# A two-layer decoder trunk on one core: one convolution put off less, another not at all, and one pair of sevens less in two down panels

## The chip, the cores and the metric

The kernel runs on one NeuronCore of a Trainium2 chip. Its engines work side by side, each through its own list of instructions: TensorE (PE in the profile; PEld is its weight load) multiplies matrices, VectorE (DVE) and ScalarE (ACT) do elementwise work, GpSimd (POOL) and SyncE (SP) issue transfers. The metric is the device time of one execution in microseconds (us), as the median of several.

## The reference

What is computed is a trunk of two layers over 256 tokens of width 2048, in float32. The first layer mixes the tokens with gated linear attention, the second with forgetting attention, and both attend to 256 memory tokens. After the mixer, each layer runs the same feed-forward block, and the change lies in that block alone:

```python
def causal_dwconv(u, w, b):
    s_ = u.shape[1]
    up = jnp.pad(u, ((0, 0), (CONV_WIDTH - 1, 0), (0, 0)))
    return w[0] * up[:, 0:s_] + w[1] * up[:, 1:s_ + 1] + w[2] * up[:, 2:s_ + 2] + b

def conv_ffn(h, w_up, conv_w, conv_b, w_down):
    u = causal_dwconv(h @ w_up, conv_w, conv_b)
    a, val = split_cols(u, [FFN_HIDDEN, FFN_HIDDEN])
    return (jax.nn.silu(a) * val) @ w_down
```

The hidden width is 5632, which is 44 chunks of 128. `w_up` is 2048 x 11264 and `w_down` 5632 x 2048, for each of the two layers.

## The kernel before

**Numbers in two parts.** Each float32 operand is split into a high part that the matmul takes as it is, and a low part, the rest. A product is three matmuls (high with high, low with high, high with low). Inputs are kept split. Weights are split as they come in: SP loads a unit of 128 x 1024 into a slot `raw`, ScalarE copies it to a slot `whi` (line 256), VectorE subtracts to get `wlo` (line 257). The slots form rings, in the feed-forward block eight for `raw` and six each for `whi` and `wlo`, so a split of a later unit has to wait until TensorE has used up an older one. Some slots are lent and carry other names (`moremk`, `moremv`, `more`).

**Panels and steps.** An "up" panel j makes four chunks of the hidden width (j to j+3) for both halves: 16 units, one for each chunk of the input. A "down" panel takes the finished chunks of one part and adds to two of the four 512-wide quarters of the output. The parts are chunks 0 to 15, 16 to 27 and 28 to 43 (`PARTS`, line 33), so down panels have 16, 12 and 16 units. The order in each layer is: up 0, 4, 8, 12 and, one panel ahead, up 16; two down panels of the first part; up 20, 24 and, ahead, up 28; two down panels of the second part; up 32, 36, 40; then the last part's down panels. The two down panels of a part are the wide ones: f = 0 for the first half of the output, f = 2 for the second. A step is one unit, and an ordinary one is 12 matmuls of 128 x 512.

**Pairs of sevens.** `pair_steps` (line 408) can take two neighbouring units together with seven block products instead of eight, in the manner of Strassen and Winograd: 21 matmuls in place of 24. For that it needs sums of the two input chunks (`usum` and `dsum`, made once) and of the weights. The weights of a pair are four splits, one of 512 and three of 1024 columns (`split_more`, lines 404 and 405), and four differences on VectorE (lines 461 to 464); two of the four splits wait for them. The seven products are collected in other banks than the ordinary ones, and after the last pair of a panel they are added to the result (`early`; for a down panel three additions and five that go to x, lines 1372 to 1382). Each up panel has a pair at chunk 6 and those of `MORE_IN` another. In down panels the chunks 4, 10, 20 and 34 begin a pair (`SEVEN_DOWN`, line 36). `ONCE` (line 43) picks which pair the first wide panel of a part takes: chunk 10 in the first part, chunk 20 in the second. The second wide panel takes all pairs of its part: 4 and 10 in the first part, 20 in the second.

**The convolution.** It runs along the tokens, while the up panel leaves the tokens in the partitions. So each half panel (`turn`, line 1481) is transposed in blocks on VectorE, sent to DRAM and fetched back on POOL's queue (lines 674 and 679), and only then convolved: 12 taps on ScalarE (line 1442), two additions (line 1449), the gate (line 1455), the product (line 1462) and the split into the chunk's two parts (lines 552 and 553), which writes the ring `m` of 16 chunks. These are listed as small steps with a cost each, 10.2 for a half panel and 20.4 for a panel. `tick` (line 1504) is called after each unit: it adds a share to a credit (1.45, in up panels with two pairs 1.7; a step of a pair counts as a tick but adds nothing) and issues steps in order while the credit lasts. A half panel's steps come due a number of ticks after its up panel: 8, or 7 for the first half where the next up panel has two pairs. `PUT_OFF` (line 42) replaces that number for panels 16 and 28, with 30 and 22. For panel 16 some delay is needed: its chunks go into the places of chunks 0 to 3 in the ring, which the first part's down panels still read, as their first four units. Panel 28's chunks go into places that the second part does not read.

**Order.** The program's order is rearranged by a planner that simulates the engines; the splits of weights have 300 instructions of priority (`AHEAD`, line 50), so they are issued well before the matmuls that need them, and a tap is kept behind the last of these splits. Each engine then runs its list in order.

Of the kernel before, what the change touches and what calls it, by code (L numbers as in the profile page):

```python
# [38 lines left out]
SCRATCH = 2048  # L39
SLOTS = 5  # L40
RAW_GUESTS = 3
PUT_OFF = {16: 30, 28: 22}
ONCE = {0: 10, 1: 20}


LEVELS = (64, 16, 4)
# [105 lines left out]
def _trunk(ctx: ExitStack, tc: tile.TileContext, xt, xtok, memt, wp, wgu, gns, gfin, cnv, par, msk, out):  # L152
# [367 lines left out]
    def add_to(f):  # L520

        return lambda b, a: V.tensor_tensor(x[f][:, b, :], x[f][:, b, :], a, ALU.add)
# [847 lines left out]
    def down_pair(l, p, f, src, sums, flip, pool, temps, then=None):  # L1370

        def early(bank):
            t0, t1 = temps()
            S.activation(t0, bank["p1"], AF.Copy)
            add_to(f)(0, t0)
            V.tensor_tensor(t0, bank["p6"], t0, ALU.add)
            V.tensor_tensor(t1, bank["p7"], t0, ALU.add)
            add_to(f)(1, t1)
            add_to(f + 1)(1, t1)
            add_to(f + 1)(1, bank["p5"])  # L1380
            V.tensor_tensor(t0, bank["p5"], t0, ALU.add)
            add_to(f + 1)(0, t0)

        def late(b, h, a):
            held_back = then is not None and h and not b and then.rooms is not None
            with tc.issue_after(then.turned[-1].ins) if held_back else nullcontext():
                add_to(f + h)(b, a)
            if then is not None:
                then(f + h, b)

        return pair_steps(where["down", l, p, f], src, sums, flip, pool, early, late)
# [26 lines left out]
    def ffn(l, nx, h, m, more, ys, zs, landing, then, pool, temps, last=None, spare=None):  # L1418
        with tc.tile_pool(name=f"ffn{l}", bufs=1) as fp:
# [14 lines left out]
            count = [0, 0, 0]  # L1434
            sums = {}
# [45 lines left out]
            def turn(j, wait):  # L1481

                count[0] += 1
                slot = count[0] % 2
                y, z = ys[slot], zs[slot]

                def evac(b, a):
                    with tc.high_priority(offset=AHEAD):
                        turned_last[0] = V.transpose(y[:, :, :, b, :], a.rearrange("p (k c i) -> p c k i", c=4, i=32))
                    if b:  # L1490
                        away = far_away(dram, flat(y), T, nc.gpsimd)
                        back = lambda: away(flat(z))
                        steps = [(0.5, lambda s=s, c=c, i=i: tap_of(j, s, c, i, slot)) for n in ((1, 2), (0,))
                                 for s in range(2) for c in range(2) for i in n]
                        steps += [(1.0, lambda: add_tap(1)), (1.0, lambda: add_tap(2)), (0.5, silu),
                                  (1.0, lambda: gated(j, 0)), (0.7, lambda: gated(j, 1))]
                        returns.append((clock[0] + 3, slot, back, [(clock[0] + wait, *step) for step in steps]))

                return evac
# [4 lines left out]
            def tick(share):  # L1504

                clock[0] += 1
                credit[0] = min(credit[0], 0.0) + share
                while returns and returns[0][0] <= clock[0] and not unread[returns[0][1]]:
                    _, slot, back, steps = returns.pop(0)
                    back()  # L1510
                    unread[slot] = 12
                    waiting.extend(steps)
                while waiting and waiting[0][0] <= clock[0] and credit[0] > 0:
                    _, cost, step = waiting.pop(0)
                    credit[0] -= cost
                    step()

            def up_pair(j):

                count[2] += 1  # L1520
                second = j // 4 in MORE_IN
                turns = [turn(j + 2 * h_, PUT_OFF.get(j) or (7 if not h_ and j // 4 + 1 in MORE_IN else 8)) for h_ in range(2)]
                u = {}
# [27 lines left out]
            def drive(steps, share=1.45):  # L1551
                for k in steps:
                    tick(share if k >= 0 else 0.0)

            def drive_up(j):
                drive(up_pair(j), 1.7 if j // 4 in MORE_IN else 1.45)
# [6 lines left out]
            for p, (lo, hi) in enumerate(PARTS[:-1]):  # L1563
                while done < hi + 4:
                    drive_up(done)
                    done += 4
                src = [m[c % RING] for c in range(lo, hi)]
                for f in (0, 2):
                    count[2] += 1
                    drive(down_pair(l, p, f, src, {c - lo: t for c, t in sums.items() if f or c == ONCE[p]}, count[2] % 2, pool,  # L1570
                                    lambda: (temps(0), temps(1))))
                sums.clear()
            lo, hi = PARTS[-1]
# [3 lines left out]
            p = len(PARTS) - 1  # L1577
            src = [m[c % RING] for c in range(lo, hi)]
# [86 lines left out]
    with tc.tile_pool(name="stash", bufs=1) as st:  # L1665
        vt = st.tile([P, 2, FOX_H * HD], F32, name="fvt")
        turned3 = vt.rearrange("p b t -> p (b t)").rearrange("p (f q k b j) -> p f q k b j", f=3, q=4, k=4, b=2)
        turned3 = [turned3[:, f] for f in range(3)]

        with tc.tile_pool(name="turn1", bufs=1) as tp:  # L1670
            n2, then = preparing("kv", bufB, tp, dram, turned3, "raw2", nc.gpsimd)
            ys = [const.tile([P, 4, 4, 2, 32], F32, name="yu", tag=tag) for tag in ("mk0", "mv0")]
            fixed = [vt.rearrange("p b t -> p (b t)")[:, 2048 + 512 * i : 2560 + 512 * i] for i in range(2)]

            def temps(i):
                return fixed[i] if i < 2 else tp.tile([P, 512], F32, name="temp", tag=f"temp{i}")

            more = []
            for t, tag in ((mk, "mk1"), (mv, "mv1")):
                parked.append(dram.tile([P, 4 * T], F32, name="park" + tag, tag="park" + tag, bufs=1))  # L1680
                nc.gpsimd.dma_start(parked[-1], t[1].rearrange("p a b -> p (a b)"))
                more.append(const.tile([P, NUNIT], F32R, name="more" + tag, tag=tag))
            ffn(0, n, bufB, bufA, more, ys, turned3, ys, then, tp, temps)
        fox(n2, vt, turned3)
# [9 lines left out]
    with tc.tile_pool(name="store", bufs=1) as op:  # L1694
# [16 lines left out]
        def then(f, b):  # L1711
            fin.add(f, b)
            if f == 0 and b == 0:
                S.activation(junk, fin.sums[:, 0, 0:1], AF.Sqrt)
            V.tensor_tensor(x[f][:, b, :], x[f][:, b, :], gf[f], ALU.mult)
# [37 lines left out]
        then.begin, then.rooms = begin, None  # L1753
        more = [op.tile([P, NUNIT], F32R, name=f"more{i}") for i in range(2)]
        ffn(1, n, bufA, bufB, more, ys, zs, zs, then, op, temps, last, spare)


# [68 lines left out]
```

## Time and profile before

| | |
|---|---|
| median of 3 runs | 2220.16 us (2220.07 to 2223.7) |
| the profiled execution's own time | 2225.07 us |
| its span, first to last instruction | 2223.3 us |
| busy: TensorE, VectorE, ScalarE, GpSimd | 99%, 83%, 65%, 6% |
| first feed-forward block, up to the last wide panel | from 456.6 to 1083.1 us of the span |
| second feed-forward block, the same | from 1502.2 to 2126.0 us |

The profile is that of one execution, so its stretches add up to its span, and not to the median. TensorE's busy share is counted from modelled ends of overlapping matmuls; whether it stood still is better seen in the time from one matmul's start to the next. In the rows of the profile, "out<-in" names what an instruction writes and reads, a number after x is a count, and square brackets give the idle time of the engine before the instruction with what ended it.

### The profile page before, as it was taken

Reading aid. Unit: us, or ns where it says so; the run is one execution under the profiler, and the core shown is the slowest. Engines: PE = TensorE matmul, PEld = TensorE weight load, DVE = VectorE, ACT = ScalarE, POOL = GpSimd, SP = SyncE. Lnnn points to the kernel's source line nnn. Section 1 sums busy time; section 2 is a strip of 40 time slices with the busy share of each in tenths; the row PEclk is TensorE's granted clock in tenths of the full one; section 3 lists DMA queues with packets and bytes.
Section 4 is the critical chain, followed back from the end, with each engine's and each line's share of the span. In section 5 each row is a group of like instructions: output and inputs, shape, how many; then the busy total and the mean of one; then the engine's idle time right before and its main releaser. Section 6 shows DMA issues by size and latency. Waiting matters only on the chain.

```text
span 2223.3 us, 30061 instructions
## 1 busy us (share of the span) xinstructions
PE 2198.0 (99%) x10273; PEld 1840.9 (83%) x10273; DVE 1853.4 (83%) x2771; ACT 1440.0 (65%) x2292; POOL 136.7 (6%) x257
## 2 busy tenths in 40 slices
PE   9999999999999999999999999999999999999998
PEld 7888888888888878887788998888888887888786
DVE  7768976689998889899887669668999888989896
ACT  6655655557784667656865555455887466766784
POOL 0000000001100000001110000000101000100100
PEclk9999999999999999999999999999999999999999
DMA  9766667777776567656777767776787657675682
GB/s 366 252 224 214 201 208 232 249 236 248 256 261 218 184 213 269 220 196 232 259 230 245 226 201 244 226 243 230 257 272 235 221 166 256 225 243 200 237 285 93
DMA packets 166289, 515.40 MB, mean 232 GB/s; under 512 B 20780, under 2 KB 42552, under 8 KB 166136
## 3 DMA queue, kind: packets, MB, share of 16 engines
q1 hardware_dynamic: 149064, 460.99, 61.9%
q0 software_dynamic: 16496, 51.71, 7.3%
q8 instruction: 80, 1.31, 0.2%
q10 hardware_dynamic: 576, 0.79, 0.1%
q14 instruction: 73, 0.60, 0.1%
HBM read 469.62 MB, written 43.79 MB: 231 GB/s over the span
## 4 chain that ended last, share of the span: by engine, by line
PE 92%; DVE 3%; ACT 2%; DMA 2%; issue 1%; POOL 0%; DVEq 0%; ACTq 0%; POOLq 0%
PE acc L361 26%; PE acc L434 26%; PE ps_s L434 14%; PE ps_o L434 7%; PE ps_t L434 6%; PE acc L332 3%; PE acc L287 3%; PE ps_s L361 2%; PE acc L391 2%; PE acc L285 1%; DMA raw<-wp 1%; ACT whi L256 1%; DVE wlo L257 1%; DVE wlo L405 1%; ACT tap L1442 1%
## 5 line engine op out<-in xcount | busy, mean ns | idle before, releaser
L257 DVE TENSOR_TENSOR wlo<-raw,whi 128x1024 fp32r<-128x1024 f32 (+2 forms) x610 | 725.6, 1198 | 198.3 <-ACT whi L256 181.0
L256 ACT ACTIVATE whi<-raw 128x1024 fp32r<-128x1024 f32 (+2 forms) x610 | 629.6, 1043 | 402.9 <-PE acc L361 141.6
L361 PE MATMUL acc<-whi,B 128*128 128x512 f32 (+3 forms) x1248 | 290.8, 369 | 0.0
L361 PEld LDWEIGHTS acc<-whi,B 128*128 128x128 f32 x1248 | 226.8, 188 | 28.1
L405 DVE TENSOR_TENSOR wlo<-raw,whi 128x1024 fp32r<-128x1024 f32 (+1 forms) x164 | 176.5, 1084 | 35.9 <-ACT whi L404 22.9
L404 ACT ACTIVATE whi<-raw 128x1024 fp32r<-128x1024 f32 (+1 forms) x164 | 154.6, 949 | 75.8 <-PE acc L434 20.4
L434 PE MATMUL acc<-whi,B 128*128 128x512 f32 x654 | 175.2, 390 | 1.4 <-ACT whi L256 1.4
L434 PE MATMUL acc<-whi,mix 128*128 128x512 f32 x620 | 163.9, 390 | 0.3 <-ACT whi L256 0.3
L361 PE MATMUL acc<-wlo,B 128*128 128x512 f32 (+3 forms) x624 | 159.0, 369 | 0.0
L434 PEld LDWEIGHTS acc<-whi,B 128*128 128x128 f32 x654 | 122.4, 188 | 28.4 <-ACT whi L256 2.9
L434 PEld LDWEIGHTS acc<-whi,mix 128*128 128x128 f32 x620 | 116.0, 188 | 26.0 <-ACT whi L256 2.0
L1442 ACT ACTIVATE tap<-fvt,cw 128x256 f32<-128x256 f32 x264 | 122.5, 530 | 17.7 <-DMA fvt<-far 10.8
L1442 ACT ACTIVATE tap<-yzu,cw 128x256 f32<-128x256 f32 x264 | 122.5, 529 | 16.8 <-DMA yzu<-far 10.0
L361 PEld LDWEIGHTS acc<-wlo,B 128*128 128x128 f32 x624 | 114.2, 188 | 14.7
L1449 DVE TENSOR_TENSOR tap<-tap,tap 128x1024 f32<-128x1024 f32 x88 | 106.8, 1214 | 0.0
L434 PE MATMUL ps_s<-whi,mix 128*128 128x512 f32 x360 | 103.9, 389 | 0.0
L434 PE MATMUL acc<-wlo,B 128*128 128x512 f32 x327 | 99.9, 390 | 0.8 <-DVE wlo L257 0.8
L434 PE MATMUL acc<-wlo,mix 128*128 128x512 f32 x310 | 92.8, 390 | 1.5 <-DVE wlo L257 1.5
L434 PE MATMUL ps_s<-whi,B 128*128 128x512 f32 x278 | 80.6, 389 | 0.0
L434 PEld LDWEIGHTS ps_s<-whi,mix 128*128 128x128 f32 x360 | 67.6, 188 | 14.0
L434 PEld LDWEIGHTS acc<-wlo,B 128*128 128x128 f32 x327 | 61.2, 188 | 14.2 <-DVE wlo L257 1.6
L361 PE MATMUL acc<-whi,mix 128*128 128x512 f32 x280 | 70.2, 390 | 0.0
(557 smaller groups left out, 4317.9 us busy)
## 6 DMA issues: line engine op xcount, KB each, us to landing
raw<-wp SPq DMA_DIRECT2D x741, 512.0 KB, 4.5
fvt<-far POOLq DMA_DIRECT2D x100, 128.0 KB, 4.9
raw<-wp SPq DMA_DIRECT2D x32, 384.0 KB, 3.6
far<-yu POOLq DMA_DIRECT2D x22, 512.0 KB, 3.6
far<-yzu POOLq DMA_DIRECT2D x22, 512.0 KB, 3.4
yzu<-far POOLq DMA_DIRECT2D x88, 128.0 KB, 4.4
raw<-wp SPq DMA_DIRECT2D x24, 388.0 KB, 3.6
x<-xtok SPq DMA_DIRECT2D x8, 512.0 KB, 7.1
```

The costliest lines, as they stand in the source:

```text
L256: casts.append(S.activation(hi[:, s], raw[:, s], AF.Copy))
L257: lows.append(V.tensor_tensor(lo[:, s], raw[:, s], hi[:, s].bitcast(F32), ALU.subtract))
L285: mm = TE.matmul(acc[p][c][:, :T], w[:, s], both[:, 0, :], start=False, stop=end and j == 3)
L287: mm = TE.matmul(acc[p][c], w[:, s], both, start=u == j == 0, stop=end and j == 3)
L332: mm = TE.matmul(acc[b][:, :n], src[kcs[j] - base][:, part, b * P : (b + 1) * P], w, start=u == 0 and low == part == j == 0, stop=u == end ...
L361: mm = TE.matmul(acc[b][:, :n], src[kc - base][:, part, b * P : (b + 1) * P], ready[low][:, j * room : j * room + n], start=i == low == pa ...
L391: mm = TE.matmul(acc[b][:, :n], src[kc - base][:, part, b * P : (b + 1) * P], w, start=i == low == part == j == 0, stop=i == end and low = ...
L404: casts.append(S.activation(hi[:, :n], src, AF.Copy))
L405: lows.append(V.tensor_tensor(lo[:, :n], src, hi[:, :n].bitcast(F32), ALU.subtract))
L434: r = TE.matmul(bank[name], x, w, start=name not in begun, stop=last)
L1442: S.activation(by_run(taps[i][:, s, c, i:]), zs[slot][:, :, 2 * c + s], AF.Copy if i else AF.Identity, bias=0.0 if i else w[3], scale=w[2 ...
L1449: V.tensor_tensor(taps[0], taps[0], taps[n][:, :, :, :T], ALU.add)
```

## The change

Panel 28 is no longer put off, so its convolution comes due at 7 and 8 ticks like any other. Panel 16's comes due at 21 ticks instead of 30. The rule for the pairs becomes symmetric: the first wide panel takes the pairs in `FIRST_DOWN`, the second takes those that are not in it. So the first part's second wide panel keeps the pair at chunk 4 and loses the one at chunk 10; the second part's first wide panel loses its only pair, at chunk 20, and its second one keeps it. The third part is as before. This holds for both layers.

```diff
-PUT_OFF = {16: 30, 28: 22}
-ONCE = {0: 10, 1: 20}
+PUT_OFF = {16: 21}
+FIRST_DOWN = (10,)
...
                 for f in (0, 2):
                     count[2] += 1
-                    drive(down_pair(l, p, f, src, {c - lo: t for c, t in sums.items() if f or c == ONCE[p]}, count[2] % 2, pool,
+                    drive(down_pair(l, p, f, src, {c - lo: t for c, t in sums.items() if (c in FIRST_DOWN) == (f == 0)}, count[2] % 2, pool,
                                     lambda: (temps(0), temps(1))))
```

## The prediction

> **What bounds the kernel now.** I read the page first, then the matmul starts of line 434 panel by panel, then the instructions around the places where TensorE stood.
>
> ```profile
> span 2223.3 us, 30061 instructions
> PE 2198.0 (99%) x10273; PEld 1840.9 (83%) x10273; DVE 1853.4 (83%) x2771; ACT 1440.0 (65%) x2292; POOL 136.7 (6%) x257
> PE 92%; DVE 3%; ACT 2%; DMA 2%; issue 1%; POOL 0%; DVEq 0%; ACTq 0%; POOLq 0%
> ```
>
> TensorE is on 92% of the chain that ended last so a time saved on VectorE (DVE) or ScalarE (ACT) counts only where TensorE waits for it. To find such places I cut both feed-forward stages at the first matmul of each panel, counting matmuls in program order (12 for an ordinary weight unit, 21 for a pair of sevens), and asked for the busy time in each stretch. The rows are, for the first layer: up 16; the two down panels of the first part; up 20, 24, 28; the two down panels of the second part; up 32, 36, 40. Then, for the second layer, up 20, 24, 32, 36, 40. The first figure after each stretch is its length; the PEld count is its matmuls; the granted clock is 1.00 throughout.
>
> ```profile
> core 0: us, PE busy (x) PEld busy (x) DVE busy (x) ACT busy (x) POOL busy (x), PEclk, DMA share, GB/s
> 626.81:669.65 42.84, 42.84 (x190) 35.47 (x189) 38.94 (x51) 35.05 (x59) 5.49 (x10) 1.00 0.74 244
> 669.65:712.49 42.84, 42.84 (x190) 35.47 (x189) 37.45 (x48) 20.90 (x25) 5.47 (x10) 1.00 0.74 247
> 712.49:754.65 42.16, 42.16 (x187) 34.91 (x186) 33.53 (x37) 26.47 (x36) 0.00 (x0) 1.00 0.54 175
> 754.65:799.42 44.77, 42.81 (x188) 34.67 (x186) 37.02 (x46) 27.39 (x40) 0.00 (x0) 1.00 0.52 180
> 799.42:843.59 44.17, 42.81 (x187) 34.70 (x186) 38.87 (x46) 31.52 (x48) 5.52 (x10) 1.00 0.75 241
> 843.59:885.75 42.16, 42.16 (x187) 34.91 (x186) 40.27 (x54) 30.47 (x45) 5.49 (x10) 1.00 0.73 257
> 885.75:917.71 31.96, 31.96 (x142) 26.46 (x141) 31.96 (x40) 21.66 (x32) 5.47 (x10) 1.00 0.75 262
> 917.71:949.67 31.96, 31.96 (x142) 26.46 (x141) 25.90 (x33) 21.66 (x33) 0.00 (x0) 1.00 0.51 180
> 949.67:993.14 43.47, 42.72 (x188) 34.75 (x186) 38.82 (x48) 27.54 (x39) 0.00 (x0) 1.00 0.59 196
> 993.14:1037.15 44.01, 42.87 (x187) 34.67 (x186) 38.48 (x45) 32.17 (x50) 5.49 (x10) 1.00 0.72 240
> 1037.15:1083.05 45.90, 43.20 (x187) 34.52 (x186) 41.73 (x55) 31.41 (x48) 5.47 (x10) 1.00 0.71 247
> ...
> 1800.67:1844.03 43.36, 42.81 (x187) 34.68 (x186) 37.01 (x46) 27.18 (x39) 0.00 (x0) 1.00 0.55 184
> 1844.03:1888.18 44.15, 42.77 (x187) 34.75 (x186) 38.89 (x46) 31.76 (x48) 5.52 (x10) 1.00 0.73 241
> 1994.26:2037.60 43.34, 42.59 (x188) 34.76 (x186) 38.82 (x48) 27.53 (x39) 0.00 (x0) 1.00 0.56 195
> 2037.60:2080.29 42.69, 42.48 (x187) 34.83 (x186) 38.47 (x45) 32.14 (x50) 5.47 (x10) 1.00 0.74 250
> 2080.29:2126.02 45.73, 43.20 (x188) 34.52 (x186) 41.86 (x55) 31.43 (x48) 5.49 (x10) 1.00 0.70 251
> ```
>
> A panel that never stands takes 42.16 us for 186 matmuls (up 28), 42.84 for 189, 31.96 for 141: 0.2267 us a matmul each time. The excess over that pace is the stall. All four down panels have none, though VectorE is busy for all 31.96 us of one of them. Up 20 has 44.77 - 42.16 = 2.61 us and up 32 has 1.31; in the second layer 1.20 and 1.18. These are the two panels that come after a put-off convolution: 6.30 us together. Up 24 has 2.01 and 1.99, up 36 has 1.85 and 0.53 (6.38 together), up 40 has 3.74 and 3.57 (7.31).
>
> How up 20 stalls is seen in the order of the instructions on ScalarE and on VectorE there (start, length, engine, line; in brackets the idle time before it and what ended that):
>
> ```profile
> 771.22 1.05 ACT L404 ACTIVATE moremk<-raw 128x1024 fp32r<-128x1024 f32 x1
> 779.30 1.06 ACT L256 ACTIVATE whi<-raw 128x1024 fp32r<-128x1024 f32 x1 [7.02 <-PE ps_s L434]
> 780.27 1.04 ACT L256 ACTIVATE moremk<-raw 128x1024 fp32r<-128x1024 f32 x1
> 781.21 1.04 ACT L404 ACTIVATE whi<-raw 128x1024 fp32r<-128x1024 f32 x1
> ...
> 773.40 1.22 DVE L1449 TENSOR_TENSOR tap<-tap,tap 128x1024 f32<-128x1024 f32 x1
> 777.12 0.69 DVE L463 TENSOR_TENSOR raw<-raw 128x512 f32<-128x512 f32 x1
> 780.39 1.23 DVE L257 TENSOR_TENSOR wlo<-raw,whi 128x1024 fp32r<-128x1024 f32 x1 [2.58 <-ACT whi L256]
> 781.54 0.68 DVE L464 TENSOR_TENSOR raw<-raw 128x512 f32<-128x512 f32 x1
> ```
>
> TensorE is in a pair of sevens and wants the split of line 404, which needs the four weight differences of lines 461 to 464. Convolution additions (line 1449) stand ahead of those on VectorE, so they run late; ScalarE's order has put two splits of later units (line 256) ahead of line 404, and the first of these waits for a slot that TensorE itself must free. A late VectorE thus costs TensorE up to 2.6 us although VectorE has 7 us idle in that panel.
>
> **The change, part by part.** *Pairs of sevens.* Each layer loses one pair in the first part's second down panel (chunk 10, so 186 matmuls become 189) and one in the second part's first (chunk 20, 141 become 144). From the rows, a panel with one pair less is 42.84 - 42.16 = 0.68 us longer. Four times that is **+2.72 us**, on the engine that sets the end, with nothing to hide it.
>
> *What the pairs cost beside TensorE.* Per pair, splits in three thousands and a five hundred and four differences go, two ordinary splits come:
>
> ```profile
> L257 DVE TENSOR_TENSOR wlo<-raw,whi 128x1024 fp32r<-128x1024 f32 x174 | 209.5, 1216 | 33.1 <-ACT whi L256 30.7 <-ACT tap L1442 1.7
> L405 DVE TENSOR_TENSOR wlo<-raw,whi 128x1024 fp32r<-128x1024 f32 x62 | 75.2, 1216 | 18.4 <-ACT whi L404 10.6 <-PE acc L434 3.4 <-PE ps_s L434 3.3
> L464 DVE TENSOR_TENSOR raw<-raw 128x512 f32<-128x512 f32 x25 | 17.2, 686 | 0.3
> ```
>
> VectorE: 3 x 1.216 + 0.69 + 4 x 0.686 - 2 x 1.216 = 4.6 us less (the short split taken as one short difference). The second part's first down panel has no pair left, so the whole early evacuation of its seven sums goes too, eight half-size additions of about 0.69, another 5.5 us. Both panels have no stall now, so **0** is gained there; the room matters only for what moves in. That more weight units are now ordinary moves no more bytes: a pair loads two units as well.
>
> *The convolution of panel 16.* It comes due at tick 21 instead of 30. Counted through, that is after the fourth step of the second down panel: three taps there, then (the two steps of the pair allow none) ten ticks of 1.45, so 16 of its 20.4 units of cost lie in that panel and 4.4 in the first three steps of up 20; before, some 6 and 14. *The convolution of panel 28* comes due at ticks 7 and 8 instead of 22: it begins in the first down panel behind the rest of panel 24's and ends in the second; up 32 then holds none, where it held some 14 of 20.4. The taps on ScalarE (line 1442) show how it lies now, in the first part's second down panel, up 20, the second part's second down panel and up 32:
>
> ```profile
> 712.49:754.65 42.16, 6.85 (x15) 1.00 0.54 175
> 754.65:799.42 44.77, 4.35 (x9) 1.00 0.52 180
> 917.71:949.67 31.96, 6.87 (x15) 1.00 0.51 180
> 949.67:993.14 43.47, 4.34 (x9) 1.00 0.59 196
> ```
>
> Of each 24 taps 9 are left for the up panel, and with them the additions, products and splits. The transfers through DRAM and POOL's queue stay at tick 3; the loads on SP only follow the slots. What receives the work has cover: the first part's second down panel then is a panel with one pair and a convolution, like up 16 (38.94 us of VectorE, 35.05 of ScalarE in 42.84, stall 0). The second part's first panel drops about 10 us of VectorE and takes under half a convolution. If that cover failed, the nearest price from above is up 40's 3.74; I take 0, since up 16 and all four down panels stand there.
>
> What up 20 and up 32 do with two pairs and next to no convolution, no row shows. From above it is what they do now (6.30 in all); from below it is 0, as no stall can be negative. The first part's second down panel has two pairs and a late start of the convolution, and no stall; up 28 has two pairs with even more beside them, and none. I take 0: **-6.30 us**.
>
> Sum: 2.72 - 6.30 = **-3.58 us**. The profiled execution took 2225.07 us, 1.8 beyond its span, so it would become 2221.5. The median of the runs is 2220.16, 4.9 below the profiled one; with the same difference, **2216.6**. Part of that 4.9 may be stalls that only profiled executions have, which would cut the gain.
>
> A rule on the pace: the Trainium skill, "TensorE: Matmul & The Clock Gate", section "Wait — 56ns, not 53.3ns?", gives 215.7 ns between warm matmuls of 512 columns. By it the twelve matmuls would add an estimated 2.59 us and the sum would be -3.71; the rows here have 226.7 ns, and they decide.
>
> **The rivals.** *The relief goes on (faster).* Up 24 and up 36 follow directly on the two panels that are cleared. If their stalls come from that neighbour's lateness, 6.38 more goes: 2.72 - 6.30 - 6.38 = -9.96, 2210.2 us. For it: up 28 carries the same load as up 24 without a stall. Against it: their own cause shows as a wait of ScalarE for a convolution block to land, which the change leaves where it is:
>
> ```profile
> 819.22 4.79 ACT L1442 ACTIVATE tap<-fvt,cw 128x256 f32<-128x256 f32 x11 [3.31 <-DMA fvt<-far]
> ```
>
> *The stalls stay (the change doesn't do what it says).* If two pairs in one panel make the bad order on ScalarE by themselves, up 20 and up 32 keep 6.30 and only the matmuls count: +2.72, 2222.9 us. For it: every stalled panel has two pairs, and up 28 with more work has none, so load alone does not decide. Against it: VectorE's additions stand right ahead of the late differences.
>
> *The stall follows the convolution (slower).* Place: the pair at steps five and six of each second down panel, which then meets the moved taps and additions. An engine that runs its orders in turn, with a tap waiting for its block or an addition ahead of the differences, would hold TensorE as in up 20. Price: the same 6.30, hence +2.72; with up 40's 7.31 in its place +3.73, 2223.9 us. From 3.58 us of new stalls on the kernel is slower than before. Against it: the blocks' transfers are issued long before,
>
> ```profile
> 895.69 2.18 POOL L679 DMA_DIRECT2D fvt<-far  x4 [2.90 <-ACT moremk L404]
> 908.99 2.18 POOL L679 DMA_DIRECT2D fvt<-far  x4 [10.56 <-ACT tap L1442]
> ```
>
> and the taps of panel 28 queue behind the end of panel 24's convolution, which shares their three buffers. For it stands the Trainium skill, "TensorE: Matmul & The Clock Gate", opening table: ScalarE and VectorE take their instructions strictly in order. The 7.02 us in which ScalarE stood at line 256 with line 404 behind it agree.
>
> **How the numbers follow.** A measurement of this kernel tells about 0.2%, 4.4 us, from no change. The forecast has 0.46: its own range goes from 2214.8 (up 36's 1.85 goes too) to 2219.7 (half of the 6.30 stays), so 0.13 of it lies below 2215.7 and counts as faster, 0.33 as the same. The relief that goes on has 0.24, faster. The stalls that stay have 0.14, the same. The stall that follows has 0.16: 0.06 the same, 0.10 slower, with more than up 40's price. Faster 0.37, same 0.53, slower 0.10. The range runs from 2208.5, just beyond the first rival, to 2223.5, between the prices of the last; some 0.07 lies below it and 0.08 above.
>
> **What would show it.** In the changed profile the two down panels count 189 and 144 matmuls and last 42.84 and 32.64 us; up 20 and up 32 last about 42.2, with at most a few taps in up 20 and none of panel 28's in up 32; up 24, 36 and 40 are about as now. A down panel longer than its pace shows the last rival, up 20 still near 44.8 the second, up 24 at 42.2 the first. The forecast is wrong if the cleared panels find another bad order, or if unprofiled executions never had these stalls.

## The result, and the profile after

The changed kernel takes 2210.36 us (median of 4 runs, 2208.87 to 2212.15), the kernel before 2221.93 us beside it (4 runs, 2220.07 to 2224.88). The ratio is 0.9947, with a 95% interval of 0.993 to 0.9964: 11.6 us or 0.53% faster, three times the 3.58 us of the forecast and a little past the first rival's 9.96.

The profiled execution took 2209.92 us where before's took 2225.07, so the two profiles differ by 15.2 us and the medians by 11.6; before's profiled execution was its slowest of those shown. The sums below are sums of the profiles.

The page of the changed kernel, and busy time by stretch, cut as in the prediction. The rows are the first part's second down panel, up 20, 24, 28, the second part's two down panels, up 32, 36, 40 and the last wide panel in the first layer; then up 20, 24, 32, 36, 40 in the second.

```profile
span 2208.0 us, 30096 instructions
PE 2194.4 (99%) x10285; PEld 1845.4 (84%) x10285; DVE 1832.8 (83%) x2731; ACT 1436.7 (65%) x2282; POOL 136.9 (6%) x257
...
712.27:755.11 42.84, 42.84 (x190) 35.48 (x189) 36.90 (x43) 30.25 (x47) 0.00 (x0) 1.00 0.60 198
755.11:797.27 42.16, 42.16 (x187) 34.92 (x186) 34.01 (x40) 22.86 (x25) 0.00 (x0) 1.00 0.62 199
797.27:839.43 42.16, 42.16 (x187) 34.92 (x186) 36.57 (x45) 32.24 (x50) 5.53 (x10) 1.00 0.71 231
839.43:881.59 42.16, 42.16 (x187) 34.92 (x186) 42.00 (x54) 35.23 (x57) 5.48 (x10) 1.00 0.73 246
881.59:914.23 32.64, 32.64 (x145) 27.04 (x144) 24.82 (x29) 22.24 (x38) 5.46 (x10) 1.00 0.78 260
914.23:946.19 31.96, 31.96 (x142) 26.47 (x141) 31.84 (x43) 19.07 (x27) 0.00 (x0) 1.00 0.68 223
946.19:988.35 42.16, 42.16 (x187) 34.92 (x186) 33.18 (x38) 22.86 (x25) 0.00 (x0) 1.00 0.61 201
988.35:1030.51 42.16, 42.16 (x187) 34.92 (x186) 37.15 (x44) 33.23 (x53) 5.52 (x10) 1.00 0.77 234
1030.51:1074.16 43.65, 42.76 (x187) 34.76 (x186) 41.12 (x52) 33.66 (x53) 5.48 (x10) 1.00 0.73 236
1074.16:1136.05 61.89, 61.89 (x275) 51.26 (x274) 54.04 (x65) 41.22 (x66) 5.49 (x10) 1.00 0.73 244
...
1793.41:1835.57 42.16, 42.16 (x187) 34.91 (x186) 34.01 (x40) 22.86 (x25) 0.00 (x0) 1.00 0.62 200
1835.57:1877.73 42.16, 42.16 (x187) 34.91 (x186) 38.01 (x47) 32.56 (x50) 5.51 (x10) 1.00 0.74 240
1984.49:2026.65 42.16, 42.16 (x187) 34.91 (x186) 34.22 (x39) 22.85 (x25) 0.00 (x0) 1.00 0.64 209
2026.65:2068.81 42.16, 42.16 (x187) 34.91 (x186) 37.69 (x44) 33.57 (x53) 5.53 (x10) 1.00 0.74 243
2068.81:2112.68 43.87, 42.77 (x188) 34.76 (x186) 41.08 (x52) 33.75 (x53) 5.49 (x10) 1.00 0.69 227
```

The down panels are at their pace, with 189 and 144 matmuls, though VectorE is busy for 31.84 of 31.96 us in one. Up 20, 24, 32 and 36 stand nowhere in either layer. Up 40 keeps 43.65 - 42.16 = 1.49 and 1.71 us, where it had 3.74 and 3.57, and the last wide panel has none, where by the same count it had 1.24 and 1.88. All stalls of the two blocks, each stretch less 0.2267 us a matmul, fall from 23.7 to 6.1 us: 17.6 less, of which 2.7 is paid for twelve matmuls. That is 14.9 of the 15.3 us between the spans.

Why up 24 is free, though the forecast left it alone, shows in VectorE's list where up 20 ends: first before (end at 799.42), then after (797.27).

```profile
803.47 0.70 DVE L1489 STREAM_TRANSPOSE yu<-fvt 128x512 f32<-128x512 f32 x1
```

```profile
797.61 0.70 DVE L1489 STREAM_TRANSPOSE yu<-fvt 128x512 f32<-128x512 f32 x1
```

The first transpose stood 4.05 us behind the panel's end and now stands 0.34 us behind it. What is sent to DRAM and fetched for the convolution lands earlier within up 24. ScalarE still waits for it, but less and earlier, and seven taps instead of eleven stand in one row ahead of the pair's splits:

```profile
813.20 2.91 ACT L1442 ACTIVATE tap<-fvt,cw 128x256 f32<-128x256 f32 x7 [2.77 <-DMA fvt<-far]
816.02 1.05 ACT L404 ACTIVATE moremk<-raw 128x1024 fp32r<-128x1024 f32 x1
```

They begin 15.9 us into the panel, and before 19.8. In all profiles here the two go together, in both layers: the first transpose behind up 20 starts 4.05 us late in the two kernels whose up 24 stalls without added work, and 0.09 to 0.34 us late in those whose up 24 is free.

### The profile page after: what moved, and what is told of

Its sections match the earlier page's. It is cut to its first block, busy times and chain, and to the rows that moved or that the text cites. A ratio compares the mean times of both kernels' runs of the same rounds, so it can differ in the third digit from the quotient of the medians.

```text
span 2208.0 us, 30096 instructions
## 1 busy us (share of the span) xinstructions
PE 2194.4 (99%) x10285; PEld 1845.4 (84%) x10285; DVE 1832.8 (83%) x2731; ACT 1436.7 (65%) x2282; POOL 136.9 (6%) x257
## 4 chain that ended last, share of the span: by engine, by line
PE 97%; DMA 1%; DVE 1%; ACT 1%; issue 0%; SPq 0%; DVEq 0%; ACTq 0%
PE acc L434 28%; PE acc L361 26%; PE ps_s L434 15%; PE ps_o L434 7%; PE ps_t L434 7%; PE acc L332 3%; PE acc L287 3%; PE ps_s L361 2%; PE acc L391 2%; PE acc L285 1%; DMA raw<-wp 1%; PE ps_s L1059 0%; DMA far<-blk 0%; DVE wlo L405 0%; PE ps_o L725 0%
## 5 line engine op out<-in xcount | busy, mean ns | idle before, releaser
L256 ACT ACTIVATE whi<-raw 128x1024 fp32r<-128x1024 f32 (+2 forms) x613 | 636.3, 1044 | 371.3 <-PE acc L361 146.0
L404 ACT ACTIVATE whi<-raw 128x1024 fp32r<-128x1024 f32 (+1 forms) x154 | 146.9, 957 | 121.0 <-PE ps_t L434 42.1
L405 DVE TENSOR_TENSOR wlo<-raw,whi 128x1024 fp32r<-128x1024 f32 (+1 forms) x154 | 167.7, 1091 | 20.8 <-ACT whi L404 12.4
L434 PE MATMUL acc<-whi,mix 128*128 128x512 f32 x668 | 171.9, 390 | 0.4 <-ACT whi L256 0.2
L434 PE MATMUL acc<-whi,B 128*128 128x512 f32 x650 | 170.2, 389 | 0.0
L434 PEld LDWEIGHTS acc<-whi,mix 128*128 128x128 f32 x668 | 125.2, 188 | 27.4 <-ACT whi L256 0.9
L434 PE MATMUL ps_s<-whi,mix 128*128 128x512 f32 x332 | 92.3, 389 | 0.0
L434 PEld LDWEIGHTS acc<-wlo,mix 128*128 128x128 f32 x334 | 62.7, 188 | 13.4 <-DVE wlo L405 0.4
L434 PEld LDWEIGHTS ps_s<-whi,mix 128*128 128x128 f32 x332 | 62.3, 188 | 12.9
```

The lines of the kernel that those rows point to most:

```text
L256: casts.append(S.activation(hi[:, s], raw[:, s], AF.Copy))
L404: casts.append(S.activation(hi[:, :n], src, AF.Copy))
L405: lows.append(V.tensor_tensor(lo[:, :n], src, hi[:, :n].bitcast(F32), ALU.subtract))
L434: r = TE.matmul(bank[name], x, w, start=name not in begun, stop=last)
```

## The experiments

Edits are shown against the changed kernel. All have their time beside runs of the kernel before; its medians there were 2223.5 to 2223.9.

**The pairs alone, the times alone.** Two kernels take one half of the change each.

```diff
-PUT_OFF = {16: 21}
+PUT_OFF = {16: 30, 28: 22}
```

> Only the pairs of sevens are those of the changed kernel; panels 16 and 28 are put off by 30 and 22 ticks as before. Theory C (the convolution that stands in up 20 and up 32 makes VectorE late there, and the lateness is handed on): the stalls of up 20, 24, 32, 36 and 40 stay near 2.6, 2.0, 1.3, 1.9 and 3.7 us, the first transpose after up 20 stays some 4 us behind the panel's end, and the twelve more matmuls make it about 2.7 us slower than before, near 2224.6. Theory P (the room that the removed pairs leave on VectorE does it, whatever the convolution's time): the stalls go and the time is near the changed kernel's 2210.

```diff
-FIRST_DOWN = (10,)
+ONCE = {0: 10, 1: 20}
...
-... if (c in FIRST_DOWN) == (f == 0)} ...
+... if f or c == ONCE[p]} ...
```

> Only the convolutions' times are those of the changed kernel (panel 16 at 21 ticks, panel 28 not put off); the pairs are those of before, so two in the first part's second down panel and one in each of the second part's. Theory C: the stalls go as in the changed kernel and the twelve matmuls are saved, so about 2.7 us faster than the changed kernel, near 2207.6. Theory P: VectorE is overfull in the second part's first down panel (busy all of 31.96 us already before), the stalls of up 20 to 40 stay or move into the down panels, and the time is near the 2222 of before or above.

The pairs alone take 2214.68 us (ratio 0.9956, 0.9941 to 0.9971), the times alone 2219.71 (0.9982, 0.9973 to 0.9992). Theory C falls in its plain form: with the pairs alone, up 20 to 36 are free although their convolutions stand where they stood. Theory P falls for the up panels: with the times alone, the same four panels are free although every pair is there. It did name the place where the times alone lose, the second part's first down panel, which keeps its pair and gets panel 28's convolution:

```profile
757.67:799.83 42.16, 42.16 (x187) 34.91 (x186) 38.28 (x46) 23.42 (x28) 0.00 (x0) 1.00 0.62 222
799.83:841.99 42.16, 42.16 (x187) 34.91 (x186) 37.37 (x46) 32.22 (x50) 5.54 (x10) 1.00 0.76 238
...
884.15:921.29 37.14, 33.67 (x143) 27.45 (x141) 30.56 (x38) 24.20 (x39) 5.49 (x10) 0.95 0.70 226
```

These are up 20, up 24 and that down panel with the times alone: 37.14 us for 141 matmuls is 5.2 us of stall, and 5.8 in the second layer, where the down panel behind it loses 0.8 more. But VectorE is not overfull there, as P has it. ScalarE waits for a block of the convolution to land, does ten taps, and only then the pair's split, with which VectorE's idle time of 6.58 us ends, and TensorE's wait of 3.86 us from start to start:

```profile
904.94 4.29 ACT L1442 ACTIVATE tap<-fvt,cw 128x256 f32<-128x256 f32 x10 [5.68 <-DMA fvt<-far]
909.13 1.04 ACT L404 ACTIVATE whi<-raw 128x1024 fp32r<-128x1024 f32 x1
910.20 1.23 DVE L405 TENSOR_TENSOR wlo<-raw,whi 128x1024 fp32r<-128x1024 f32 x1 [6.58 <-ACT whi L404]
```

**One panel's time alone.** The pairs of the change, with only one of the two times.

```diff
-PUT_OFF = {16: 21}
+PUT_OFF = {16: 21, 28: 22}
```

> The changed kernel, but panel 28 put off by 22 ticks as before. Theory C: up 20 and up 24 are free of stalls in both layers, up 32, 36 and 40 keep theirs (1.3, 1.9, 3.7 and 1.2, 0.5, 3.6 us): of before's stalls 2.6 + 2.0 + 1.2 + 2.0 = 7.8 go, 2.7 is paid for the matmuls, so about 5 us below before, near 2217. Theory P: as the changed kernel, near 2210.

```diff
-PUT_OFF = {16: 21}
+PUT_OFF = {16: 30}
```

> The changed kernel, but panel 16 put off by 30 ticks as before. Theory C: up 20 and up 24 keep their stalls (2.6, 2.0 and 1.2, 2.0 us), up 32 and 36 have none and up 40 is as in the changed kernel: about 7.8 us above the changed kernel, near 2218. Theory P: as the changed kernel, near 2210.

They take 2215.16 us (0.9962, 0.9948 to 0.9976) and 2210.62 (0.9943, 0.9928 to 0.9958). With the pairs gone, panel 16's time doesn't matter: at 30 ticks up 20 and up 24 are free, and the kernel is as fast as the changed one. Panel 28's does: put off by 22, up 32 and 36 are free, but the last wide panel stalls by 6.4 and 2.8 us. Neither theory had that place.

**Where the pair stands.** A new theory, L, for the first part: VectorE comes late into up 20 because two things meet at the end of the panel before, the adding up of the last pair's products and the put-off convolution. So I left the count of pairs as in the run with the pairs alone, and moved the one pair from chunk 4 to chunk 10.

```diff
-PUT_OFF = {16: 21}
+PUT_OFF = {16: 30, 28: 22}
...
-... if (c in FIRST_DOWN) == (f == 0)} ...
+... if c == (10 if p == 0 else 20 * (f > 0))} ...
```

> As the run with the pairs alone (put-off 30 and 22 as before, one pair in the first part's second down panel, none in the second part's first), but that one pair is chunk 10 instead of chunk 4, so its products are added up near the panel's end. Theory L (VectorE's work at the panel's end, the adding up beside the put-off convolution, makes it late for the pairs of up 20): the first pair's differences in up 20 end some 11 us into the panel as before, not 3 to 4, up 20 and up 24 stall again by 1 to 2.6 us in each layer, and the time is 4 to 7 us above the pairs alone, 2219 to 2222. Theory R (one pair less is what counts, wherever it stands): as the pairs alone, 2214.7, without stalls in up 20 and 24.

2221.43 us (0.9983, 0.9974 to 0.9993). Up 20 and up 24 stall again, by 1.7 and 2.0 us in the first layer, 1.1 and 2.1 in the second, and VectorE's list in up 20 is that of before. The rows are up 20 and 24 of this run, then the first and second pair's last difference in its up 20:

```profile
755.40:799.30 43.90, 42.81 (x188) 34.69 (x187) 37.02 (x46) 27.29 (x39) 0.00 (x0) 1.00 0.55 182
799.30:843.43 44.13, 42.75 (x188) 34.76 (x186) 38.86 (x46) 31.61 (x48) 5.54 (x10) 1.00 0.77 243
...
766.41 0.69 DVE L464 TENSOR_TENSOR raw<-raw 128x512 f32<-128x512 f32 x1
781.42 0.68 DVE L464 TENSOR_TENSOR raw<-raw 128x512 f32<-128x512 f32 x1
```

The second pair's last difference starts 781.42 - 755.40 = 26.0 us into the panel; before it was 781.54 - 754.65 = 26.9. Where up 20 doesn't stall it starts earlier, by the same rows of the pairs alone (panel from 755.59), the times alone (from 757.67) and the changed kernel (from 755.11):

```profile
778.20 0.68 DVE L464 TENSOR_TENSOR raw<-raw 128x512 f32<-128x512 f32 x1
```

```profile
778.65 0.69 DVE L464 TENSOR_TENSOR raw<-raw 128x512 f32<-128x512 f32 x1
```

```profile
773.05 0.69 DVE L464 TENSOR_TENSOR raw<-raw 128x512 f32<-128x512 f32 x1
```

That is 22.6, 21.0 and 17.9 us. TensorE gets to the pair after 12 x 7 + 21 matmuls, 23.8 us, and needs the first split of the differences (line 404) 9 matmuls later, at 25.8; split and low part take some 2.3 us, so the split has to begin by about 23.5. It begins at 781.21 - 754.65 = 26.6 us in before (the prediction shows the row), at 25.7 in this run, and in time, at 21.9, with the pairs alone. ScalarE's list in this run, then with the pairs alone:

```profile
779.18 2.01 ACT L256 ACTIVATE whi<-raw 128x1024 fp32r<-128x1024 f32 x2 [6.16 <-DMA raw<-wp]
781.10 1.04 ACT L404 ACTIVATE whi<-raw 128x1024 fp32r<-128x1024 f32 x1
```

```profile
775.96 1.06 ACT L256 ACTIVATE whi<-raw 128x1024 fp32r<-128x1024 f32 x1 [5.05 <-PE ps_t L434]
776.93 0.62 ACT L1455 ACTIVATE tap<-tap 128x512 f32<-128x512 f32 x1
777.45 1.05 ACT L404 ACTIVATE whi<-raw 128x1024 fp32r<-128x1024 f32 x1
```

The last difference is a sign of the lateness and not what the split waits for: in before and in this run the split begins 0.3 us before that difference does. It reads only what lines 461 and 462 write, and these were done at 777.8 here. What it stands behind on ScalarE are two splits of later units, before the first of which ScalarE stood idle for 6.16 us. So L names rightly which two things must meet. That they act through the order which the planner then gives ScalarE, and not through VectorE's time itself, fits these rows, but no run changed that order alone.

**All pairs of the first part; all pairs with panel 28 at 14.** Two tries at a faster kernel, which also test L.

```diff
-... if (c in FIRST_DOWN) == (f == 0)} ...
+... if (c in FIRST_DOWN if f == 0 else True)} ...
```

> The changed kernel, but the first part's second down panel takes both its pairs, 4 and 10, as before. Theory L: without the put-off convolution the late adding up alone is not enough, as the run with the times alone showed; up 20 and up 24 stay free, and six matmuls less make it 1.4 us faster than the changed kernel, near 2209.0. Theory R: the second pair brings up 20's stalls back, 2.6 + 2.0 + 1.2 + 2.0 us, and it is near 2217.

```diff
-PUT_OFF = {16: 21}
+PUT_OFF = {16: 21, 28: 14}
...
-... if (c in FIRST_DOWN) == (f == 0)} ...
+... if f or c in (10, 20)} ...
```

> All pairs of before, panel 16 at 21 ticks as in the changed kernel, panel 28 at 14, so that the second part's first down panel, which stalled by 5.2 and 5.8 us with the times alone, holds a pair but none of panel 28's convolution. Theory L: that panel is free again, up 20 to 36 stay free as with the times alone, and the saved matmuls make it up to 2.7 us faster than the changed kernel, near 2208. Theory R: near before's 2222, as one pair less is what counts.

The first takes 2206.59 us (0.9919, 0.9902 to 0.9936), with up 20 to 36 free as L has it. The second takes 2211.14 (0.9939, 0.9925 to 0.9954): its down panels and up 20 to 36 are free, but the last wide panel stalls by 1.2 and 3.3 us, which eats the matmuls that it saves.

**Lateness made by hand.** Whether lateness at a panel's turn is handed on was so far read from traces alone. So I put needless work on VectorE at the end of up 20.

```diff
                     with tc.high_priority(offset=AHEAD):
+                        for _ in range(4 if j == 20 and not b else 0):
+                            V.tensor_tensor(flat(y), x[0].rearrange("p b n -> p (b n)"), x[1].rearrange("p b n -> p (b n)"), ALU.add)
                         turned_last[0] = V.transpose(...)
```

> The changed kernel with four additions of 128 x 1024 more on VectorE in each layer, just ahead of the first transpose after up 20; what they write is overwritten by the transposes, and the output is not touched. They take 4.6 us, about the lateness that before had there (4.1 against 0.3 us after the panel's end). Theory L, handed on: the convolution's blocks land later, ScalarE waits for them in up 24, and up 24 stalls by about 2 us in each layer as before, so 2 to 4 us above the changed kernel, near 2213.5. Against it: up 24's stalls in before were an accident of their own; up 24 stays at 42.16 us and the time at 2210.

2209.48 us, no change, and it says nothing: the planner moved the additions some 80 us ahead, to 715.6 us of the span, where they delay nothing, and the transposes are where they were. The second try reads the block that is about to be transposed:

```diff
                     with tc.high_priority(offset=AHEAD):
+                        for _ in range(8 if j == 20 and not b else 0):
+                            V.tensor_tensor(flat(y)[:, :512], a, a, ALU.add)
                         turned_last[0] = V.transpose(...)
```

> The changed kernel with eight additions of 128 x 512 more on VectorE in each layer, between the evacuation of up 20's first product block and its first transpose; they read that block, so they can't be moved ahead of it, and what they write is overwritten. They take 4.8 us. If lateness at a panel's turn is handed on: the first transpose after up 20 comes some 4 to 5 us after the panel's end instead of 0.3, the convolution's blocks land as much later, and up 24 stalls by about 2 us in each layer, so 2 to 4 us above the changed kernel. If up 24's stalls in before were an accident of their own: up 24 stays at 42.16 us and the time is the changed kernel's.

2218.64 us (0.998, 0.9969 to 0.9991), 8 us above the changed kernel where 2 to 4 were expected. The planner spread the eight among the splits, so the last transpose of up 20 starts 18.5 us behind the panel's end and not 4.6; the lateness is larger than the 8.8 that before had. Up 24, up 28 and ScalarE's list in up 24:

```profile
797.81:842.66 44.85, 42.83 (x187) 34.76 (x186) 35.55 (x44) 27.44 (x41) 5.52 (x10) 1.00 0.61 193
842.66:886.96 44.30, 42.46 (x187) 34.78 (x186) 41.60 (x54) 34.25 (x53) 5.50 (x10) 1.00 0.72 238
...
827.36 4.79 ACT L1442 ACTIVATE tap<-fvt,cw 128x256 f32<-128x256 f32 x11 [3.98 <-DMA fvt<-far]
832.05 1.04 ACT L256 ACTIVATE moremk<-raw 128x1024 fp32r<-128x1024 f32 x1
```

Up 20 itself is at its pace. Up 24 stalls by 2.7 us, the next panel by 2.1, and ScalarE shows the same picture as in the kernel before: a wait for the block, then eleven taps in one row ahead of the splits. TensorE's longest wait in up 24 ends at 833.15, with the split that begins at 832.05 behind those taps. Lateness is handed on, over more than one panel.

**The second part's pair.** What clears up 32 and behind? With the pairs alone, and chunk 20's pair back in the second part's first down panel:

```diff
-PUT_OFF = {16: 21}
+PUT_OFF = {16: 30, 28: 22}
...
-... if (c in FIRST_DOWN) == (f == 0)} ...
+... if c == 20 or (c in FIRST_DOWN) == (f == 0)} ...
```

> As the run with the pairs alone (put-off 30 and 22), but the second part's first down panel keeps its pair at chunk 20. If the two removed pairs act each on the up panels behind them: up 20 and 24 stay free as with the pairs alone; up 32, 36 and 40 stall as before (1.3, 1.9, 3.7 and 1.2, 0.5, 3.6 us), 12.2 us together, where the pairs alone had 0.7 there and 2.9 more than before in the last panels; with 1.4 us of matmuls saved that gives 2214.7 + 12.2 - 0.7 - 2.9 - 1.4 = 2222. If the first part's pair alone does it: near 2213.

2213.07 us (0.9951, 0.9937 to 0.9964). Up 20, 24 and 32 are free, up 36 stalls by 3.1 and 4.4, up 40 by 1.1 and 0.8. The time is that of the second case, the panels are neither's. Over all runs one pattern holds for this part. Wherever panel 28 is put off by 22, the first transpose comes 4.0 to 5.4 us behind up 32's end, and from up 32 on each layer loses 2.9 to 8.1 us, in up 32, 36, 40 or the last wide panel, differently in each kernel. Put off by 14, the transpose comes at 1.3 to 1.5 us, and 2.5 and 4.0 us are lost. Where it isn't put off, it comes at 0.1 to 0.3 us, and 0.8 to 2.8 us are lost (the two runs with added work aside).

**The faster one again, beside the changed kernel.**

> The kernel with both pairs in the first part's second down panel and the changed kernel's times, once more, beside the changed kernel on the same chip: six matmuls less, so 1.4 us below it by the matmuls; 3.8 us below it by the medians so far.

> The changed kernel once more, for the comparison on the same chip: 2210.4 us, stalls only in up 0, up 8 and up 40.

2206.54 us (0.9926, 0.9912 to 0.994) and 2210.55 us (0.9941, 0.9929 to 0.9954) on the same chip, 4.0 us apart. Six matmuls are 1.4 us; the profiles show 2.1 us less stall, in up 40 above all (0.9 and 0.9 us against 2.1 and 1.4). The first part's second down panel and up 20 of the faster kernel:

```profile
712.15:754.31 42.16, 42.16 (x187) 34.91 (x186) 35.92 (x42) 29.60 (x46) 0.00 (x0) 1.00 0.53 181
754.31:796.47 42.16, 42.16 (x187) 34.91 (x186) 38.08 (x46) 23.53 (x28) 0.00 (x0) 1.00 0.62 222
```

This is the best of the kernels here: the convolutions' times of the change, with the first part's pairs of before. The stalls and times in one view (us, first and second layer; "late pair" is chunk 10's in the first part's second down panel). The stalls are those of one profile each, and one entry differs by some 0.6 us between two profiles of the changed kernel (1.5 and 1.7, then 2.1 and 1.4). The medians were taken on four occasions, with the kernel before at 2221.9 to 2223.9 us, so a difference of 2 us between two rows says little:

| kernel | late pair | panels 16, 28 put off | up 20 + 24 | second part's down panels | from up 32 on | median |
|---|---|---|---|---|---|---|
| before | yes | 30, 22 | 4.6, 3.2 | 0, 0 | 8.1, 7.1 | 2221.9 |
| pair at chunk 10 only | yes | 30, 22 | 3.7, 3.2 | 0, 0 | 3.8, 5.6 | 2221.4 |
| the pairs alone | no | 30, 22 | 0, 0 | 0, 0 | 2.9, 3.8 | 2214.7 |
| the same, chunk 20's pair kept | no | 30, 22 | 0, 0 | 0, 0 | 4.3, 5.1 | 2213.1 |
| panel 28's time alone | no | 30, no | 0, 0 | 0, 0 | 2.6, 2.8 | 2210.6 |
| panel 16's time alone | no | 21, 22 | 0, 0 | 0, 0 | 6.5, 3.5 | 2215.2 |
| the changed kernel | no | 21, no | 0, 0 | 0, 0 | 1.5, 1.7 | 2210.4 |
| the times alone | yes | 21, no | 0, 0 | 5.2, 6.6 | 0.9, 0.8 | 2219.7 |
| all pairs, panel 28 at 14 | yes | 21, 14 | 0, 0 | 0, 0 | 2.5, 4.0 | 2211.1 |
| both pairs in the first part | yes | 21, no | 0, 0 | 0, 0 | 0.8, 1.4 | 2206.6 |

## Why the prediction was right or wrong

The direction and the range were right; the likeliest case gave 3.58 us where 11.6 were measured (15.2 between the profiles). 2210.36 lies outside that case's own 2214.8 to 2219.7: the range held because it reached past the first rival. That the rival's 2210.2 is so near is partly luck. It adds only up 24 and up 36 to the forecast, for 9.96 us in all, while stalls of up 40 and the last wide panel went as well.

*The matmuls, +2.72 us:* as worked out; the two down panels last 42.84 and 32.64 us, and the twelve matmuls are the page's 10285 - 10273.

*Up 20 and up 32, -6.30 us:* right in size, both are at 42.16 us in both layers. But the cause was too narrow. The forecast gave it all to the convolution's place. In the first part the late pair and the put-off convolution are needed both, and either half of the change clears up 20. In up 32 the convolution's place is not enough either: four kernels still put panel 28 off by 22 and have no stall in that panel.

*How up 20 stalls:* the prediction let the split of line 404 wait for all four differences. The split begins at 781.21 and the last difference at 781.54, so it waited in ScalarE's list, behind the two splits of line 256 that the same rows show. That VectorE's lateness sets this order is argued and was not shown.

*What the pairs cost beside TensorE, 0:* this step failed. It argued that a down panel without a stall has nothing to gain. The late pair stood in a panel without a stall, and moving it there, from chunk 4 to chunk 10 with all else kept, was enough to bring back stalls in the next two panels, 3.7 us in the first layer and 3.2 in the second. Of its work the adding up stands at the panel's end; that it is this part which counts was not tested by itself. With the two times as before, the removed pairs bring 2223.6 - 2214.7 = 8.9 us, 2.7 of matmuls paid.

*Up 24 and 36 as now, 0 instead of -6.38:* this step failed as well, and the first rival names what happened. The reason given against it, that their wait for a landing block is left where it is, overlooked that the block is sent when VectorE has transposed it, and VectorE was 4 us late at the panel's turn. The run with lateness made by hand shows that link at work in up 24 and up 28.

*Up 40 as now:* it lost 2.2 and 1.9 us of its stall, and the last wide panel lost 1.2 and 1.9, which the forecast had not even counted. By the table, the stalls from up 32 on fall from 15.2 us in both layers to 1.7 with the times alone and to 6.7 with the pairs alone: panel 28's time is the stronger half, but not the only one.

*The other rivals.* That the stalls stay because two pairs make the bad order by themselves: fallen, as no up panel lost its second pair and four are free. That the stall follows the convolution: not in the changed kernel, but it is what the times alone show, in the second part's first down panel instead of the place named, at 5.2 and 5.8 us instead of 6.30 for all. It takes the pair and the convolution in one panel of 31.96 us, since the pair's split stands behind taps that wait for a block, and the change removes that pair.

*Open.* Which engine's lateness puts the stall of a put-off panel 28 into up 36 in one kernel and into the last wide panel in another was not settled. Nor was what up 0 and up 8 of the second layer do: 1.2 and 1.7 us of stall in the changed kernel's profile against 0.2 and 0.4 before, in a place where nothing was edited.

## What to carry to other kernels

A panel without a stall can still be the one that makes the next panel wait: look at how far behind the panel's end each engine's last work for it stands, not only at where TensorE stands. A stall that comes when two delays add up goes with either of them, so a change that removes both looks like two gains and is one; the half that costs matmuls can be put back. And look at what stands in front of the urgent work in an engine's list: in two places here it was a convolution's taps, waiting for a block to land, that held the splits TensorE needed.

## What the runs showed of the hardware

TensorE's clock, at 1.00 in all rows of the kernel before and the changed one shown here, halves after a long wait. In the run with panel 16's time alone, the last wide panel has one wait of 3.70 us from one matmul's start to the next, in the first row here; in the second row the granted clock is 0.51, and matmuls follow each other at 0.427 us instead of 0.227 for 15 matmuls, 3.0 us more.

```profile
1095.80:1099.60 3.80, 0.49 (x3) 0.08 (x1) 1.17 (x2) 3.74 (x10) 2.19 (x4) 0.89 1.03 409
1099.60:1105.70 6.10, 6.10 (x15) 4.76 (x16) 4.62 (x6) 4.51 (x8) 0.00 (x0) 0.51 0.77 219
```

With the pairs alone, a wait of 3.04 us in the second layer's same panel leaves it at 1.00:

```profile
2136.70:2139.80 3.10, 0.45 (x3) 0.04 (x1) 1.13 (x2) 3.10 (x9) 2.15 (x4) 1.00 1.06 377
2139.80:2146.00 6.20, 6.20 (x27) 5.14 (x28) 4.72 (x6) 5.03 (x9) 0.04 (x1) 1.00 0.83 236
```

The Trainium skill, "TensorE: Matmul & The Clock Gate", section "HAM oscillation — how this bites in real kernels", says that the clock is halved when TensorE idles for more than about 3.4 us. From start to start these two waits agree, and so do waits of 3.86 and 4.27 us with the times alone, behind which matmuls follow each other at 0.43 us too. The figure is met only roughly, since the profile counts 3.31 us of the 3.70 as idle. The run with the pair at chunk 10 doesn't fit so simply: in up 36 of its second layer no wait is over 1.3 us from start to start, yet several in a row bring the clock down for some 4 us.

```profile
2060.00:2064.00 4.00, 2.98 (x11) 1.53 (x9) 2.78 (x3) 4.00 (x6) 0.00 (x0) 1.00 0.41 103
2064.00:2066.00 2.00, 1.20 (x4) 0.67 (x4) 1.85 (x2) 2.00 (x5) 0.00 (x0) 1.00 0.99 285
2066.00:2068.00 2.00, 1.91 (x5) 1.52 (x6) 1.93 (x2) 2.00 (x4) 0.00 (x0) 0.59 0.76 240
```

So of the 5 to 7 us that a bad place costs here, up to 3 can be the clock and not the wait.
